# A planned encoder kernel: new costs and a rule for the shared port in the clock that lays out the order

## The chip, the cores and the metric

The kernel runs on one core of a Trainium2 chip. The metric is the device time in microseconds of one execution; three runs of the kernel before gave 1139.76, 1140.32 and 1140.52, the median is 1140.32. A core has TensorE (PE, matmuls, with a queue of its own for weight loads), VectorE (DVE), ScalarE (ACT), GpSimd (POOL) and SyncE (SP, which here issues the DMAs and the transposes done by DMA). Each engine works through its own instructions in the order in which the program has them; engines wait for each other by semaphores.

## The reference

Two groups of 512 rows with 1024 columns, prompt and sample, go through two layers with the same weights. A layer norms its input, projects it once, feeds two mixers and projects their gated outputs back:

```python
h = rmsnorm(x, g_norm) * (1.0 + scale[:, None, :]) + shift[:, None, :]
proj = h @ w_in
qa, ka, va, ga, qb, kb, vb, gb = jnp.split(proj, idx, axis=-1)
qa = rope(...) * (HEAD_DIM ** -0.5); ka = rope(...)
for window, dilation in DILATED_PATTERNS:          # (128,1), (512,4), (2048,16)
    o_p, lse_p = dilated_attention(qa, ka, va, window, dilation)
    ...
ya = oa.reshape(B, S, A_WIDTH) * jax.nn.silu(ga)   # 8 heads of 64, softmax-merged patterns
yf = retention_direction(qf, kf, vf, lg_f, False)  # 4 heads, key 64, value 128
yb = retention_direction(qf[:, ::-1], ..., True)[:, ::-1]
r = yf + yb
r = r * lax.rsqrt(jnp.mean(r * r, axis=-1, keepdims=True) + EPS)
yr = r.reshape(B, S, R_WIDTH) * jax.nn.silu(gb)
out = jnp.concatenate([ya, yr], axis=-1) @ w_out
return x + gate[:, None, :] * out
```

A last rmsnorm follows the second layer. The inputs are float32. The kernel keeps that precision by splitting each operand into a high and a low part and multiplying three times (high·high, high·low, low·high).

## The kernel before

**Tiles.** The input projection is cut into items: P*i* (queries and keys of attention pair *i*, two heads), V*i* (its values), G*i* (a gate, eight of them), R*i* and W*i* (queries/keys and values of two retention heads). ORDER0 and ORDER1 (lines 31 and 32) fix the order of items in the two layers; this is the main flow. An item's product is a 128x512 tile in PSUM (`banks`) for each group b, made of 24 matmuls `hT,wH` and `hT,wL`. At the end of a layer stands the output projection: for each block of 128 rows, 8 parts k in the order 0, 1, 4, 5, 6, 7, 2, 3, each with the split yT (left) and wo (right), 48 matmuls `wo,yT` of 512 columns a block.

**Side work.** Beside the main flow some dozen generators wait for their turn:

- `rope` turns queries and keys and has SP write them into stacks (QS, KS, KL), 24 small DMAs per pair and group.
- `attn` (line 897) multiplies two score matmuls per tile and lets DVE take the mask and minimum (`sS<-banks,tabs`). `soften` (line 920) does the exponential on ACT, then on DVE a reciprocal, a scaling of it and, for two tiles, a TENSOR_SCALAR and a SCALAR_TENSOR_TENSOR that write the high and low half of the weights, pt. When both halves of a head are there, SP transposes the two pt into pT. `attn_pv` (line 950) multiplies pT with the values vn in 24 matmuls with 64 output rows, when both heads of a pair and group are transposed.
- `ret` and `r_out` (line 1030, line 1092) are the retention; `r_out` makes the norm (`nw`, `nwr`) with a chain of DVE operations between two groups of matmuls.
- `prepper` splits the next weights: ACT makes wH, GpSimd wL. `prep_o` does so for w_out: GpSimd makes the low part of wo, eight instructions of 128x1024 a layer.
- `splitter` makes yT: the high part on ACT, the low part on DVE, for each k and group.

**What sets the order.** The program order on each engine is the order of the Python calls. Every call goes through `Engine.__call__` (line 345 issues it), which also advances a rough clock: `Plan.note` (line 127) takes an operation's cost from `Engine.cost` (line 361), starts it when its engine, its inputs and its buffers are free in that clock, and notes the end. `Plan.pump` (line 174) runs between the main flow's groups of three matmuls: it lets every generator go on whose wish (a time in that clock) has come by the clock of PE, and else returns to the main flow. So the clock decides only what stands ahead of what; the chip's times are its own. `backlog()` lets no further score begin while the clock of DVE is over AHEAD = 3000 ns past that of PE. Buffers come from a heap of 48 tiles and are given out by the same clock; a tile's name in the trace is that of the first use of its buffer (so KS, KL or QS, sd or rsq may be names of other contents). The eight PSUM banks are five for the main flow and three for the rest.

## Time and profile before

| | |
|---|---|
| runs, median | 1140.32 us |
| profiled execution | 1136.72 us |
| its span, first to last instruction | 1135.0 us |
| mean granted TensorE clock | 0.976 |
| PE / DVE / ACT / POOL busy | 1056.1 / 853.1 / 391.4 / 201.1 us |
| instructions PE / DVE / ACT / POOL | 5443 / 1664 / 701 / 108 |

The profile gives for each engine its busy time and the intervals in which it stood, with what it waited for. A wait of PE is time that the program loses, if the work behind it isn't waiting for something else anyway; a wait of the other engines costs only where PE waits for them in turn. All instructions have line 345, because they are issued in one place, so groups are told apart by the names of their output and inputs.

### The profile page before, as it was taken

Reading aid. Unit: us, or ns where it says so; the run is one execution under the profiler, and the core shown is the slowest. Engines: PE = TensorE matmul, PEld = TensorE weight load, DVE = VectorE, ACT = ScalarE, POOL = GpSimd, SP = SyncE. Lnnn points to the kernel's source line nnn. Section 1 sums busy time; section 2 is a strip of 40 time slices with the busy share of each in tenths; the row PEclk is TensorE's granted clock in tenths of the full one; section 3 lists DMA queues with packets and bytes.
Section 4 is the critical chain, followed back from the end, with each engine's and each line's share of the span. In section 5 each row is a group of like instructions: output and inputs, shape, how many; then the busy total and the mean of one; then the engine's idle time right before and its main releaser. Section 6 shows DMA issues by size and latency. Waiting matters only on the chain.

```text
span 1135.0 us, 15575 instructions
## 1 busy us (share of the span) xinstructions
PE 1056.1 (93%) x5443; PEld 836.4 (74%) x5443; DVE 853.1 (75%) x1664; ACT 391.4 (34%) x701; POOL 201.1 (18%) x108
## 2 busy tenths in 40 slices
PE   5999999999999999939999999999999999995997
PEld 4677776677876778617888878877797777773886
DVE  5688766689768996885457798599858995598555
ACT  5454314223242333442233343424143232363101
POOL 3153002121012011260000111103203011233000
PEclk9999999999999999969999999999999999997999
DMA  9905977338775677793222396247742484765232
GB/s 282 325 20 142 179 183 245 113 105 181 160 180 196 165 159 158 188 234 91 92 81 69 91 200 137 75 103 170 144 122 51 118 179 104 201 143 154 75 111 74
DMA packets 256509, 164.53 MB, mean 145 GB/s; under 512 B 162032, under 2 KB 225808, under 8 KB 256432
## 3 DMA queue, kind: packets, MB, share of 16 engines
q1 hardware_dynamic: 256432, 163.55, 57.2%
q8 instruction: 43, 0.70, 0.3%
q14 instruction: 34, 0.28, 0.1%
HBM read 79.59 MB, written 8.40 MB: 78 GB/s over the span
## 4 chain that ended last, share of the span: by engine, by line
PE 54%; DVE 31%; SPq 5%; DMA 5%; issue 2%; ACT 2%; DVEq 0%; ACTq 0%
PE banks L345 54%; DVE pt L345 10%; SPq L345 5%; DVE sd L345 3%; DVE sS L345 3%; DVE sm L345 2%; DVE rc L345 2%; DVE rsq L345 2%; DVE th L345 1%; DVE yr L345 1%; DMA wa<-in_w_ada_dram 1%; DMA pT<-pt 1%; DVE nw L345 1%; DVE hT L345 1%; DMA raw<-in_w_in_dram 1%
## 5 line engine op out<-in xcount | busy, mean ns | idle before, releaser
L345 PE MATMUL banks<-hT,wH 128*128 128x512 f32 x1536 | 482.6, 395 | 3.5 <-DVE sm L345 2.3
L345 PEld LDWEIGHTS banks<-hT,wH 128*128 128x128 f32 x1536 | 288.1, 189 | 79.4 <-issue 15.0
L345 PE MATMUL banks<-hT,wL 128*128 128x512 f32 x768 | 300.4, 391 | 0.0
L345 POOL TENSOR_TENSOR wL<-raw,wH 128x512 fp32r<-128x512 f32 (+1 forms) x80 | 149.8, 1888 | 739.6 <-ACT wH L345 545.3
L345 PE MATMUL banks<-wo,yT 128*128 128x512 f32 (+1 forms) x792 | 182.1, 391 | 35.7 <-DVE yT L345 23.6
L345 PEld LDWEIGHTS banks<-wo,yT 128*128 128x128 f32 x792 | 148.0, 192 | 67.6 <-DVE yT L345 24.5
L345 PEld LDWEIGHTS banks<-hT,wL 128*128 128x128 f32 x768 | 145.2, 189 | 30.8
L345 PE MATMUL banks<-wH,hT 128*128 128x256 f32 x512 | 96.3, 283 | 0.0
L345 PEld LDWEIGHTS banks<-wH,hT 128*128 128x128 f32 x512 | 81.4, 191 | 1.9 <-issue 0.8
L345 ACT ACTIVATE wH<-raw 128x512 fp32r<-128x512 f32 (+1 forms) x80 | 61.3, 794 | 46.4 <-DMA raw<-in_w_in_dram 29.4
L345 PE MATMUL banks<-wL,hT 128*128 128x256 f32 x256 | 72.4, 283 | 0.0
L345 ACT ACTIVATE sS<-sS,sm 128x512 f32<-128x512 f32 x67 | 47.8, 714 | 67.8 <-DVE sm L345 67.7
L345 DVE SCALAR_TENSOR_TENSOR pt<-sS,sm,pt 128x512 f16<-128x512 f32 x67 | 64.8, 967 | 2.9
L345 DVE TENSOR_TENSOR res<-banks,gb 128x512 f32<-128x512 f32 (+1 forms) x33 | 22.1, 671 | 47.3 <-PE banks L345 47.3
L345 DVE TENSOR_SCALAR pt<-sS,sm 128x512 f16<-128x512 f32 x67 | 50.5, 753 | 7.7 <-DMA pT<-pt 6.2
L345 PE MATMUL banks<-sr,rv 128*128 128x512 f32 x167 | 48.9, 399 | 3.9 <-ACT sr L345 2.6
L345 DVE CUSTOM_DVE_ANT_0 sS<-banks,tabs 128x512 f32<-128x512 f32 x67 | 43.1, 685 | 10.8 <-PE banks L345 10.8
L345 POOL TENSOR_TENSOR wo<-rawo,wo 128x1024 fp32r<-128x1024 f32 x16 | 39.9, 2518 | 56.7 <-PE banks L345 28.8
L345 PEld LDWEIGHTS banks<-wL,hT 128*128 128x128 f32 x256 | 49.0, 191 | 1.0
L345 PE MATMUL banks<-pT,vn 128*64 128x512 f16 x384 | 46.2, 390 | 0.2 <-DMA vn<-vt 0.2
L345 ACT ACTIVATE sq<-xr 128x1024 bf16<-128x1024 f32 (+2 forms) x15 | 14.2, 943 | 88.0 <-issue 43.2
L345 PE MATMUL banks<-wa,siluT 128*32 128x128 f32 (+1 forms) x384 | 33.0, 397 | 8.7 <-DVE nst L345 6.0
(304 smaller groups left out, 1393.3 us busy)
## 6 DMA issues: line engine op xcount, KB each, us to landing
raw<-in_w_in_dram SPq DMA_DIRECT2D x56, 512.0 KB, 5.3
wa<-in_w_ada_dram SPq DMA_DIRECT2D x48, 512.0 KB, 4.9
rawo<-in_w_out_dram SPq DMA_DIRECT2D x16, 512.0 KB, 4.7
QS<-rs SPq DMA_DIRECT2D x96, 64.0 KB, 2.0
KL<-rc SPq DMA_DIRECT2D x74, 64.0 KB, 2.0
KS<-rs SPq DMA_DIRECT2D x70, 64.0 KB, 2.0
x1d<-xr SPq DMA_DIRECT2D x8, 512.0 KB, 2.9
xr<-x1d SPq DMA_DIRECT2D x8, 512.0 KB, 3.9
```

Of the source, the lines that this page charges most:

```text
L345: r = fn(*args, **kw)
```

## The change

`Engine.cost` gets other numbers: 512-column matmuls of TensorE 228 ns instead of 216 (64-row ones lose 14 ns); DVE operations from SBUF get 65 ns for each input that is one element wide; GpSimd 30 + 2.37 n instead of 150 + 2.1 n. And `note` gets a rule, `held`: an operation of DVE without a PSUM operand may not overlap in the clock with one of GpSimd, and the other way round; the later starts when the earlier has ended. AHEAD, the order of items, the buffers and the computations are as they were, and each engine has as many instructions as before.

```diff
--- before.py
+++ after.py
@@ -96,6 +96,7 @@
     def __init__(self):
         self.free = {"PE": 0.0, "DVE": 0.0, "ACT": 0.0, "POOL": 0.0, "SP": 0.0}
         self.dma = 0.0
+        self.port = {"DVE": [], "POOL": []}
         self.ready = {}
         self.last = {}
         self.slots = {}
@@ -124,7 +125,18 @@
         t = self.at(*tiles)
         return 0.0 if t <= self.free[eng] else t
 
-    def note(self, eng, cost, outs, ins, nbytes=0.0):
+    def held(self, eng, start, cost):
+
+        other = self.port["POOL" if eng == "DVE" else "DVE"]
+        for s, e in other:
+            if s < start + cost and e > start:
+                start = e
+        own = self.port[eng]
+        own.append((start, start + cost))
+        del own[:-64]
+        return start
+
+    def note(self, eng, cost, outs, ins, nbytes=0.0, port=False):
         part = eng == "SP" and outs[0].shape[0] < P
         outs = [k for a in outs for k in self.keys(a)]
         ins = [k for a in ins for k in self.keys(a)]
@@ -136,6 +148,8 @@
                 start = max(start, self.seen(eng, self.last.get(k)))
         if self.dead.intersection(outs + ins):
             raise RuntimeError("use of a spare buffer")
+        if port:
+            start = self.held(eng, start, cost)
         end = start + cost
         self.free[eng] = end
         if eng == "SP":
@@ -354,7 +368,9 @@
             nbytes = 0.0
             if self.name == "SP":
                 nbytes = outs[0].free_size() * outs[0].shape[0] * (2.0 / 290.0 if outs[0].dtype == F16 else 4.0 / 360.0)
-            self.plan.note(self.name, self.cost(op, outs, ins), outs, ins, nbytes)
+            psum = any(a.tensor.name.startswith("banks") for a in ins)
+            port = self.name == "POOL" or (self.name == "DVE" and not psum)
+            self.plan.note(self.name, self.cost(op, outs, ins), outs, ins, nbytes, port)
             return r
         return call
 
@@ -372,18 +388,21 @@
                     return max(4 * c, 60.0)
                 self.strip = out.offset // out.ap[0][0] // 32
                 return 27.0 if self.strip > last >= 0 else 4 * c
-            return 0.5 * c + 14.0 if out.shape[0] == 64 else c
+            return 0.5 * c if out.shape[0] == 64 else c + 12.0
         if self.name == "DVE":
             wide = [a for a in ins if a.free_size() > 1]
             fast = len(wide) <= 1 and not psum and op != "tensor_reduce"
             if op == "tensor_reduce":
                 n = wide[0].free_size()
-            return 66.0 + n * (0.53 if fast else 1.05) + (60.0 if fast and len(ins) > 1 and n > 64 else 0.0)
+            extra = 0.0
+            if n > 64 and not psum and (op == "scalar_tensor_tensor" or fast):
+                extra = 65.0 * sum(1 for a in ins if a.free_size() == 1) + (60.0 if fast else 0.0)
+            return 66.0 + n * (0.53 if fast else 1.05) + extra
         if self.name == "ACT":
             extra = sum(1 for a in outs[1:]) + sum(1 for a in ins if a.free_size() == 1)
             return (53.0 if psum else 93.0) + 93.0 * extra + 0.833 * n
         if self.name == "POOL":
-            return 150.0 + 2.1 * n
+            return 30.0 + 2.37 * n
         if op == "dma_start_transpose":
             return 1250.0 * n / 1024
         return 450.0 if any("dram" in str(a.tensor.name) for a in ins + outs) else 650.0
```

What moves, at three places. At the end of layer 0, TensorE's rows before (`hT,wH` are projections of the main flow, `KS,KL` here two scores of pair 3, `wo,yT` the first part of the output projection, and `pT,vn` the first of 24 matmuls of attn_pv for pair 3, group 0):

```order
L345 MATMUL banks<-hT,wL 128x512
L345 MATMUL banks<-KS,KL 128x512 x2
L345 MATMUL banks<-hT,wH 128x512 x2
L345 MATMUL banks<-hT,wL 128x512
L345 MATMUL banks<-hT,wH 128x512 x2
L345 MATMUL banks<-hT,wL 128x512
L345 MATMUL banks<-wo,yT 128x512 x6
L345 LDWEIGHTS vn
L345 MATMUL banks<-pT,vn 64x512
```

All other scores of pair 3, and attn_pv of pair 2, stand ahead of these rows. In the changed order the last projections are followed by two scores of pair 3, group 0, and attn_pv of pair 2, group 1, begins:

```order
L359 MATMUL banks<-hT,wH 128x512 x2
L359 MATMUL banks<-hT,wL 128x512
L359 MATMUL banks<-KS,KL 128x512 x2
L359 LDWEIGHTS vn
L359 MATMUL banks<-pT,vn 64x512
```

Behind its 24 matmuls stand 22 score matmuls of pair 3 (14, then 8 in rows with QS), and only then attn_pv of pair 3, group 0, whose first rows end this piece:

```order
L359 LDWEIGHTS vn
L359 MATMUL banks<-pT,vn 64x512
L359 MATMUL banks<-KS,KL 128x512 x14
L359 MATMUL banks<-QS 128x512
L359 MATMUL banks<-KL,QS 128x512
L359 MATMUL banks<-QS 128x512
L359 MATMUL banks<-KL,QS 128x512
L359 MATMUL banks<-QS 128x512
L359 MATMUL banks<-KL,QS 128x512
L359 MATMUL banks<-QS 128x512
L359 MATMUL banks<-KL,QS 128x512
L359 LDWEIGHTS vn
```

Before, all 16 score pairs of pair 3 stood among the projections; now four do, the first of them 62 matmuls ahead of the projections' end, and twelve stand behind it.

The same place on SP's queue, before (the first rows are the end of pair 3's stacks for group 1, 24 DMAs; those for group 0 stand further up, ahead of other loads):

```order
L345 DMA KS<-rs 32x512 x4
L345 DMA KS<-rc 32x512 x4
L345 DMA_TRANSPOSE pT<-pt 128x16x128 x4
L345 DMA_TRANSPOSE vn<-vt 128x16x128
L345 DMA rawo<-in_w_out_dram 128x1024 x3
L345 DMA_TRANSPOSE pT<-pt 128x16x128 x2
L345 DMA rawo<-in_w_out_dram 128x1024 x4
L345 DMA_TRANSPOSE pT<-pt 128x16x128 x3
L345 DMA rawo<-in_w_out_dram 128x1024
L345 DMA_TRANSPOSE pT<-pt 128x16x128
```

And now (the first rows are the end of 48 DMAs in a run, group 1's stacks and behind them group 0's, issued behind attn_pv of pair 2, group 0):

```order
L359 DMA KS<-sd 32x512
L359 DMA KS<-yr 32x512
L359 DMA rawo<-in_w_out_dram 128x1024
L359 DMA_TRANSPOSE vn<-vt 128x16x128
L359 DMA rawo<-in_w_out_dram 128x1024 x4
L359 DMA_TRANSPOSE pT<-pt 128x16x128 x2
L359 DMA rawo<-in_w_out_dram 128x1024 x2
L359 DMA_TRANSPOSE pT<-pt 128x16x128 x6
```

The four transposes ahead of vn (pair 2's) are gone from behind the stacks, and six stand in one run at the end.

At the end of layer 1, TensorE's rows before (the 36 `wo,yT` are the first six parts of the first block):

```order
L345 MATMUL banks<-hT,wH 128x512 x2
L345 MATMUL banks<-hT,wL 128x512
L345 MATMUL banks<-wo,yT 128x512 x36
L345 LDWEIGHTS vn
L345 MATMUL banks<-pT,vn 64x512
```

And now, to the end of the program:

```order
L359 MATMUL banks<-hT,wH 128x512 x2
L359 MATMUL banks<-hT,wL 128x512
L359 MATMUL banks<-hT,wH 128x512 x2
L359 MATMUL banks<-hT,wL 128x512
L359 MATMUL banks<-wo,yT 128x512 x360
L359 MATMUL banks<-wo,yT 128x256 x48
```

The 24 matmuls of attn_pv for pair 3, group 1, which parted the output projection into 36 and 324, now stand among the projections.

## Rows read from the trace of the kernel before

**Rows 1.** Page, busy time, share of the span, instructions:

```profile
PE 1056.1 (93%) x5443; PEld 836.4 (74%) x5443; DVE 853.1 (75%) x1664; ACT 391.4 (34%) x701; POOL 201.1 (18%) x108
```

**Rows 2.** Page, chain that ended last, by engine:

```profile
PE 54%; DVE 31%; SPq 5%; DMA 5%; issue 2%; ACT 2%; DVEq 0%; ACTq 0%
```

**Rows 3.** Waits of PE: us in total, times, longest us:

```profile
PE banks L345 <- DVE yT L345: 23.6, 2, 13.6
...
PE banks L345 <- DVE nwr L345: 7.1, 4, 2.6
...
PE banks L345 <- DVE sm L345: 3.5, 2, 2.3
...
PE banks L345 <- ACT sr L345: 2.6, 3, 1.3
```

**Rows 4.** Timeline of PE, both seams: start, length, operation, [idle before <-releaser]:

```profile
491.59 2.93 PE L345 MATMUL banks<-wo,yT 128*128 128x512 f32 x6 [12.07 <-ACT yT L345]
...
509.51 3.78 PE L345 MATMUL banks<-wo,yT 128*128 128x512 f32 x8 [10.04 <-DVE yT L345]
513.22 3.05 PE L345 MATMUL banks<-pT,vn 128*64 128x512 f16 x24
516.20 8.00 PE L345 MATMUL banks<-wo,yT 128*128 128x512 f32 x34
...
1035.66 4.54 PE L345 MATMUL banks<-wo,yT 128*128 128x512 f32 x11 [13.57 <-DVE yT L345]
```

**Rows 5.** Stages: us, PE, PEld, DVE, ACT, POOL busy (x), PEclk, DMA share, GB/s:

```profile
479.53:491.59 12.06, 0.00 (x0) 0.00 (x0) 6.87 (x15) 5.60 (x8) 3.81 (x2) 0.65 0.98 183
...
499.47:509.51 10.04, 0.00 (x1) 0.01 (x1) 9.86 (x12) 1.72 (x3) 6.30 (x5) 0.70 0.76 210
...
1022.09:1035.66 13.57, 0.00 (x0) 0.00 (x1) 13.32 (x14) 3.79 (x7) 8.27 (x4) 0.64 0.32 61
...
233.81:237.20 3.39, 3.39 (x8) 2.71 (x9) 3.35 (x6) 0.00 (x0) 0.00 (x0) 0.51 0.24 58
```

**Rows 6.** Timeline of PE within layer 0, columns as in rows 4:

```profile
399.72 0.62 PE L345 MATMUL banks<-hT,wH 128*128 128x512 f32 x2
...
400.40 0.62 PE L345 MATMUL banks<-hT,wH 128*128 128x512 f32 x2
```

**Rows 7.** Groups of POOL by form: busy us, mean ns, idle before:

```profile
L345 POOL TENSOR_TENSOR wL<-raw,wH 128x512 fp32r<-128x512 f32 x48 | 69.5, 1470 | 262.8 <-ACT wH L345 137.3 <-PE banks L345 33.3 <-DVE sr L345 29.8
L345 POOL TENSOR_TENSOR wo<-rawo,wo 128x1024 fp32r<-128x1024 f32 x16 | 39.9, 2518 | 56.7 <-PE banks L345 28.8 <-DVE sm L345 15.3 <-ACT wo L345 10.5
```

**Rows 8.** Tile pt: ns min/median/max, first and last start:

```profile
L345 DVE TENSOR_SCALAR pt<-sS,sm x67: 474/486/2651, 95.4 to 1032.4; 128x512 f16<-128x512 f32 x67
L345 DVE SCALAR_TENSOR_TENSOR pt<-sS,sm,pt x67: 750/752/2771, 96.0 to 1032.9; 128x512 f16<-128x512 f32 x67
```

**Rows 9.** Timelines of POOL and DVE at the end of layer 0:

```profile
487.78 12.28 POOL L345 TENSOR_TENSOR wo<-rawo,wo 128x1024 fp32r<-128x1024 f32 x5 [10.50 <-ACT wo L345]
...
492.92 0.15 DVE L345 RECIPROCAL sm<-sm 128x2 f32<-128x2 f32 x1
...
497.85 2.76 DVE L345 SCALAR_TENSOR_TENSOR pt<-sS,sm,pt 128x512 f16<-128x512 f32 x1
```

**Rows 10.** Timeline of SP's queue, a stack and transposes:

```profile
428.16 2.49 SPq L345 DMA_DIRECT2D QS<-rs  x4
...
441.27 9.96 SPq L345 DMA_TRANSPOSE pT<-pt  x4
```

**Rows 11.** DMA issues: KB each, median us to landing:

```profile
QS<-rs SPq DMA_DIRECT2D x96, 64.0 KB, 2.0
...
pT<-pt SPq DMA_TRANSPOSE x64, 4.8
```

**Rows 12.** Groups of DVE by form: busy us, mean ns, idle before:

```profile
L345 DVE CUSTOM_DVE_ANT_0 sS<-banks,tabs 128x512 f32<-128x512 f32 x67 | 43.1, 685 | 10.8 <-PE banks L345 10.8
...
L345 DVE RECIPROCAL sm<-sm 128x2 f32<-128x2 f32 x64 | 10.1, 157 | 2.6 <-ACT sS L345 1.0 <-ACT th L345 0.9 <-ACT y L345 0.8
```

## The prediction

> **What bounds the kernel now.** I read the busy shares first. TensorE is busy 1056.1 us of the span of 1135.0, VectorE 853.1, GpSimd 201.1 [rows 1]: the kernel is bound by TensorE's work, and the change removes none of it. What can move is the time in which TensorE stands, some 79 us with the start. The chain that ended last has 54% on PE but 31% on DVE and 5% each on SP's queue and on DMAs [rows 2]; so in a third of the span TensorE is at the mercy of VectorE's order. The list of TensorE's waits then says where. The largest are for yT, the split operand of the output projection: 23.6 us in two waits on DVE [rows 3], and 12.07 us in one on ACT [rows 4]. The rest lies in the midst of the layers: nwr (the norm of retention) 7.1 us in four waits, sm 3.5, sr 2.6 [rows 3].
>
> The timeline and the table by stage place the long ones. At the end of layer 0 TensorE stands for 12.07 us up to 491.59 and for 10.04 up to 509.51, at the end of layer 1 for 13.57 up to 1035.66 [rows 4]. In the latter two DVE is busy for 9.86 and 13.32 us, with GpSimd beside it for 6.30 and 8.27 [rows 5]. Behind a stop TensorE is granted about half of its clock (1.2 of 2.4 GHz): 0.51 in the 3.39 us behind an nwr wait at 231 us, with eight matmuls where 0.227 us each would allow 15, so 1.6 us lost [rows 5, 6]. The spacing of 0.227 is read from the steady rows: three matmuls from 399.72 to 400.40 [rows 6].
>
> The seams' price from the same rows: layer 0 has 12.07 + 10.04 of standing, and matmuls at half clock: six in 2.93 and eight in 3.78 (0.51 and 0.48 apart, after 0.39 for the last one) lose 1.7 + 1.8. That is 25.6. Layer 1 has 13.57, and eleven in 4.54 (0.415 apart) lose 2.1: 15.7 [rows 4].
>
> Why is DVE late there? GpSimd's products (wo and wL) take 2518 and 1470 ns [rows 7]. Softening's two wide operations, both from SBUF, take 486 and 752 ns at the median, but up to 2651 and 2771 [rows 8]. The timeline shows one of them at 2.76 beside a row of wo, while a reciprocal beside the same row takes 0.15 [rows 9]. So the shared port that the change speaks of is real.
>
> **The change part by part.** No instruction is added or removed, none gets shorter. It alters four numbers of the clock that lays out the order, and adds a rule to it. The new numbers are nearer to the trace: TensorE 0.228 us for 512 columns (0.216 before; rows: 0.227), GpSimd 1.243 for 512 columns against 1470 ns, 2.457 for 1024 against 2518; the one-wide operand puts softening's operations at 462 and 669 ns against 486 and 752. The rule says that a DVE operation without a PSUM operand and a GpSimd operation never overlap. All of the effect is in what now stands ahead of what; I price it at three places.
>
> *End of layer 0.* Here the order gets worse. The 24 matmuls attn_pv(2,1), and 12 of the 16 score pairs of attention pair 3, stood among the projections; now they stand behind the last of these, in the rows shown above. Counted with 0.227, and 3.05 us for 24 attn_pv matmuls [rows 4], the projections end 24 × 0.227 + 3.05 = 8.5 us earlier, at 471.0 instead of 479.5. But pair 3's stacks (24 small DMAs per group) are now issued for both groups in one run behind attn_pv(2,0), group 1 first. That point is 150 matmuls, 34.0 us, ahead of the projections' end: 437.0. At 0.62 us an issue [rows 10] the first half of group 0's stack is the 36th: 437.0 + 22.3 + 2.0 to land [rows 11] = 461.3. Its first scores stand 62 matmuls ahead of the end, at 456.9, and TensorE waits 4.4 us. Fourteen matmuls and a gate later, at about 466, DVE starts four softenings, pair 3's two ahead of pair 2's last two. One is 2 × (0.486 + 0.752) [rows 8] + 0.157 for the reciprocal and as much for its scaling [rows 12] = 2.8 us; four end at 477, and one or two wo of 2.5 in their way make it 479.5 to 482; I take 481. Two transposes, 2.49 apart on SP's queue and 4.8 to land [rows 10, 11], bring attn_pv(2,1) to 488.3. TensorE stands from 475.4 + two scores to then, and all that follows is behind that in its order. From 491.4 DVE has 11 score operations at 0.685 = 7.5, six softenings = 16.8 and two small ones, 25.4 in all: 517, and with two to three wo between 519 to 524; I take 521. Two transposes 7.3, attn_pv(3,1) 3.05, then y and yT 2.1 and six matmuls 1.4: the first block of 48 output matmuls ends at 535. Before, it ends 30 matmuls after 516.20 [rows 4], at 523.0. So **+12 us**. The ends: if the first scores find their stack and no wo falls before attn_pv(2,1), 8 less (+4); if four more wo of 2.5 stand in DVE's way, +22.
>
> *End of layer 1.* Here it gets better. attn_pv(3,1) stood behind the first 36 output matmuls; now no attn_pv stands behind the projections at all, pair 3's scores being asked for 33 us of TensorE work sooner. Softening, which filled most of the 13.32 us of DVE in the standing window, is done by then. What is left is the last five wo, 12.6 us of GpSimd, with yT operations (0.7 alone, as the 0.685 of another 128x512 one [rows 12]) that each wait for one. Six matmuls use 1.36 us per yT where the pair of yT and wo needs 2.5: over four of them 4.6, less about 2 that begins before the projections end, plus 1 of half clock: 3.5 left of 15.7, **-12 us**. The ends: -14 (nothing left) and -5 (four alternations counted in full, 10).
>
> *Within the layers.* Of the four nwr waits two keep their place against the chain before them, the other two are given room: -1.5 of the 7.1. For sm and sr (6.1) I take a third, -2, and for the half clock behind one of the four stops -1.6: **-5**. Unknown on both sides: with all of these waits and four such stretches gone -19 at most, with each of the two kinds doubled in another place +13; I keep -12 and +6, as the waits are many and independent.
>
> Parts costed at nothing: the 64-row matmuls' 14 ns (TensorE's order is its only effect), the start (TensorE waits there for the first norms, ahead of any choice) and the end, where 324 output matmuls follow each other with DVE far ahead; if a later yT were late there, it would cost its wait in full.
>
> Sum: +12 - 12 - 5 = -5. Against the profiled execution's 1136.72 that is 1131.7; the median of the runs, 1140.32, lies 3.6 higher: **1135**.
>
> A rule speaks against the change. The Trainium skill ("SBUF — State Buffer", section "Who interferes with whom") states that a DVE instruction with at most one SBUF input, outside the two-port modes, does not contend with GpSimd. The trace agrees where a reciprocal ran in 0.15 us beside GpSimd while its neighbours took over 2 us. By that rule the new clock keeps operations waiting that the chip lets pass, and the time would be the first rival's.
>
> **Rivals.** First, *slower*: the rule charges too much. It holds every DVE operation without a PSUM operand for up to 2.457 us, reciprocals too, which the trace shows at 0.15 beside a wo [rows 9], and GpSimd in turn. DVE then looks busier than it is, the limit on DVE's backlog (AHEAD) lets pair 3's scores out later than needed, and TensorE, in order, stands behind them. For it: the late scores at the end of layer 0 are such a shift. Against: layer 1 shifts the other way. Price: three more wo of 2.5 us in layer 0, +20; two more in layer 1, -7; the rest 0: +13, 1153. It decides if attn_pv(2,1) starts after about 496.
>
> Second, *no change*: the standing only moves. TensorE's 1056 us are fixed, both layers have the same DVE work to do behind the last projections, and the waits within the layers come back elsewhere: +12 - 12 + 0, 1140.
>
> Third, *more gain*: layer 0 ends no later than before (+2), since the projections before it wait less and SP gets the stacks out sooner, layer 1 -13, within the layers -9: -20, 1120.
>
> **How the numbers follow.** The forecast (gain in layer 1, loss in layer 0, a little within) has 0.38, its own range 1129 to 1140; slower 0.30; no change 0.15; more gain 0.17. A measurement of this kernel can tell 0.2%, 2.3 us, from no change. Faster takes the third rival and 0.33 of the forecast's 0.38, 0.50; same its rival and 0.04 of the forecast, 0.19; slower the rest, 0.31. The range that leaves a tenth on each side is 1118 to 1151.
>
> **What would show it.** Right: two standing windows at the end of layer 0, the first closed by a transpose of pt for attn_pv(2,1), the end of the first 48 output matmuls some 12 us later than 523 counted from the projections' old end; a single stop of 2 to 5 us at the end of layer 1, closed by yT with wo beside it; nwr waits of about 5.5 us. Wrong: a first stop at layer 0 that ends before 482 (the stacks were not late), or one beyond 10 us at the end of layer 1 (wo, not softening, held DVE), or more waits within the layers than the 13 us of before.

## The result, and the profile after

The changed kernel takes 1179.99 us (median; 1175.90 to 1182.09) against 1140.04 for the kernel before beside it: a ratio of 1.0348 [1.0325, 1.0371]. It is slower, outside the range of 1118 to 1151. The profiled execution took 1182.09 us, with a span of 1179.9 where before had 1135.0: 44.9 us more.

The page's busy times, to be read against [rows 1]:

```profile
PE 1077.3 (91%) x5443; PEld 844.9 (72%) x5443; DVE 856.3 (73%) x1664; ACT 391.0 (33%) x701; POOL 200.7 (17%) x108
```

The work is the same. DVE and POOL differ from before by 3.2 and 0.4 us; PE shows 21 us more because more of its matmuls ran at half clock behind a stop (the granted clock over the span is 0.957; before 0.976). The waits of PE (us in total, times, longest), against [rows 3]:

```profile
PE banks L359 <- DMA pT<-pt: 31.9, 7, 16.1
PE banks L359 <- ACT sr L359: 14.4, 6, 5.1
PE banks L359 <- DMA wa<-in_w_ada_dram: 14.2, 9, 6.0
PE banks L359 <- DVE nwr L359: 5.8, 2, 3.2
PE banks L359 <- DVE sr L359: 5.6, 5, 2.0
...
PE banks L359 <- DVE yT L359: 3.9, 2, 2.6
PE banks L359 <- DVE sm L359: 2.6, 1, 2.6
```

yT has fallen from 23.6 to 3.9 and nwr from 7.1 to 5.8. In their place stand pT, the transposed softmax weights, on which no wait of TensorE ended before, and sr, the split scores of retention: 2.6 us on ACT before, 14.4 now, and 1.3 on DVE before, 5.6 now. Of the 14.2 for wa, 6.0 stand at the start, where before a wait of the same length was for nst on DVE. The timeline of PE tells where (start, length, operation, idle before and its releaser):

```profile
322.12 0.47 PE L359 MATMUL banks<-QS 128*128 128x512 f32 x1 [1.84 <-DMA QS<-rs]
324.65 0.76 PE L359 MATMUL banks<-QS,KL 128*128 128x512 f32 x1 [2.06 <-DMA KL<-rc]
330.56 1.95 PE L359 MATMUL banks<-sr,rv 128*128 128x512 f32 x3 [5.15 <-ACT sr L359]
...
496.08 0.61 PE L359 MATMUL banks<-KS,KL 128*128 128x512 f32 x2
...
513.10 1.06 PE L359 MATMUL banks<-pT,vn 128*64 128x512 f16 x4 [16.07 <-DMA pT<-pt]
515.66 4.42 PE L359 MATMUL banks<-pT,vn 128*64 128x512 f16 x19 [1.50 <-DMA pT<-pt]
...
537.29 1.06 PE L359 MATMUL banks<-pT,vn 128*64 128x512 f16 x4 [10.98 <-DMA pT<-pt]
...
887.38 1.95 PE L359 MATMUL banks<-sr,rv 128*128 128x512 f32 x3 [3.29 <-ACT sr L359]
889.12 1.05 PE L359 MATMUL banks<-KL,KS 128*128 128x512 f32 x2
891.68 1.95 PE L359 MATMUL banks<-sr,rv 128*128 128x512 f32 x3 [1.50 <-ACT sr L359]
...
900.23 1.95 PE L359 MATMUL banks<-sr,rv 128*128 128x512 f32 x3 [1.45 <-ACT sr L359]
```

The first three rows and the last four are new stops: the retention of the second pair, in layer 0 and in layer 1. In layer 1 TensorE does two score matmuls (KL, KS), waits, does three products (sr, rv), then the next two scores, with nothing else between. A round takes 4.3 us (887.38 to 891.68) where its five matmuls are worth 1.14 at [rows 6]' 0.227. The rows between are the end of layer 0, against [rows 4]. By stretches (us, busy time of PE, PEld, DVE, ACT, POOL, granted clock, DMA share, GB/s):

```profile
320.28:352.30 32.02, 18.32 (x61) 8.27 (x60) 14.76 (x20) 9.27 (x13) 4.81 (x3) 0.68 0.69 180
884.09:900.23 16.14, 8.40 (x16) 4.34 (x15) 5.99 (x9) 3.17 (x5) 1.28 (x2) 0.58 0.62 131
497.03:513.10 16.07, 0.00 (x2) 0.00 (x0) 15.47 (x20) 4.97 (x8) 7.14 (x3) 0.62 0.90 234
526.31:537.29 10.98, 0.00 (x1) 0.00 (x1) 10.56 (x25) 3.75 (x9) 1.21 (x1) 0.59 0.33 62
```

In the retention stretch of layer 1 no engine is full: DVE 5.99 of 16.14 us, ACT 3.17. TensorE is granted 0.58 there, near its half clock. It is a chain that goes round, not a busy engine. At the end of layer 0 DVE is full in both stops (15.47 of 16.07 us and 10.56 of 10.98), as it was before in two of the three at the seams [rows 5].

**Where the 45 us are.** I count as the loss of a stage the time between two fixed places of TensorE's work less what its matmuls between them take at steady spacing (0.227 us for 512 columns, half for one of attn_pv). So half clock counts as loss too. The end of a layer runs from the last gate but one to the end of the second block of the output projection; the retention stage begins with the end of the second pair's wide product (its values).

| stage | before | after | difference |
|---|---|---|---|
| second retention pair, layer 0 | 3.3 | 23.5 | +20.2 |
| end of layer 0 | 27.6 | 50.6 | +23.0 |
| second retention pair, layer 1 | -0.2 | 14.7 | +14.9 |
| end of layer 1 | 16.0 | 0.1 | -15.9 |
| all the rest | 41.5 | 44.3 | +2.8 |

The retention stage's other end isn't the next projection. Counted up to that projection's first matmul, it loses 0.5 before and 22.5 after in layer 0, and 0.0 and 15.0 in layer 1.

### The profile page after: what moved, and what is told of

Same layout as the page of the kernel before. It is cut to its first block, busy times and chain, and to the rows that moved or that the text cites. A ratio compares the mean times of both kernels' runs of the same rounds, so it can differ in the third digit from the quotient of the medians.

```text
span 1179.9 us, 15588 instructions
## 1 busy us (share of the span) xinstructions
PE 1077.3 (91%) x5443; PEld 844.9 (72%) x5443; DVE 856.3 (73%) x1664; ACT 391.0 (33%) x701; POOL 200.7 (17%) x108
## 4 chain that ended last, share of the span: by engine, by line
PE 54%; DVE 24%; SPq 11%; DMA 7%; issue 2%; ACT 1%; DVEq 0%; ACTq 0%
PE banks L359 54%; SPq L359 11%; DVE pt L359 8%; DMA wa<-in_w_ada_dram 2%; DVE sS L359 2%; DVE yr L359 2%; DVE th L359 2%; DMA raw<-in_w_in_dram 2%; DMA pT<-pt 2%; DVE rc L359 2%; DVE rs L359 1%; DVE sm L359 1%; DVE rsq L359 1%; DVE sd L359 1%; DVE sr L359 1%
## 5 line engine op out<-in xcount | busy, mean ns | idle before, releaser
L359 PE MATMUL banks<-wo,yT 128*128 128x512 f32 (+1 forms) x712 | 161.4, 385 | 5.7 <-DVE yT L359 3.9
L359 PEld LDWEIGHTS banks<-wo,yT 128*128 128x128 f32 x712 | 130.7, 189 | 32.8 <-DVE yT L359 4.8
L359 ACT ACTIVATE sS<-sS,sm 128x512 f32<-128x512 f32 x84 | 59.9, 714 | 71.4 <-DVE sm L359 71.3
L359 PE MATMUL banks<-pT,vn 128*64 128x512 f16 x384 | 53.5, 422 | 32.6 <-DMA pT<-pt 31.9
L359 DVE SCALAR_TENSOR_TENSOR pt<-sS,sm,pt 128x512 f16<-128x512 f32 x84 | 75.0, 893 | 5.1 <-PE banks L359 1.6
L359 PE MATMUL banks<-sr,rv 128*128 128x512 f32 x158 | 52.8, 437 | 20.0 <-ACT sr L359 14.4
L359 PEld LDWEIGHTS <-vn 128*64 128x64 f16 x384 | 23.9, 119 | 59.2 <-issue 44.3
L359 DVE CUSTOM_DVE_ANT_0 sS<-banks,tabs 128x512 f32<-128x512 f32 x84 | 54.4, 687 | 15.9 <-PE banks L359 15.2
L359 PEld LDWEIGHTS banks<-sr,rv 128*128 128x128 f32 x158 | 30.4, 202 | 35.5 <-ACT sr L359 19.1
L359 PE MATMUL banks<-wa,siluT 128*32 128x128 f32 (+1 forms) x384 | 37.5, 410 | 14.4 <-DMA wa<-in_w_ada_dram 14.2
```

What stands on the lines that cost most here:

```text
L359: r = fn(*args, **kw)
```

## The experiments

The table has every kernel that was run, with the losses of those four stages. "Apart" is what the order says of retention: how many TensorE matmuls stand between a score and its own product, in the four rounds of the first head of group 0. "pv" is the number of attn_pv matmuls that stand behind the layer's last projection.

| kernel | us | ratio to before | apart, layer 0 | loss | pv | end 0 | apart, layer 1 | loss | pv | end 1 |
|---|---|---|---|---|---|---|---|---|---|---|
| before | 1140.04 | | 24 37 44 45 | 3.3 | 48 | 27.6 | 28 31 32 18 | -0.2 | 24 | 16.0 |
| after | 1179.99 | 1.035 | 0 0 6 3 | 23.5 | 72 | 50.6 | 0 0 0 0 | 14.7 | 0 | 0.1 |
| pe_cost_only | 1160.06 | 1.017 | 25 32 33 13 | 4.2 | 72 | 39.3 | 25 28 29 18 | -0.1 | 0 | 0.2 |
| costs_only | 1184.35 | 1.039 | 2 5 29 15 | 30.7 | 72 | 40.8 | 25 28 29 18 | -0.1 | 0 | 4.7 |
| rule_only | 1161.79 | 1.019 | 37 19 26 27 | 0.1 | 96 | 61.2 | 16 19 53 39 | 0.3 | 24 | 13.3 |
| rule_holds_dve_only | 1145.48 | 1.006 | 13 16 17 6 | 14.1 | 48 | 29.6 | 21 17 5 3 | 7.9 | 0 | 0.1 |
| old_costs_ahead_2500 | 1156.11 | 1.014 | 25 28 29 6 | 5.9 | 48 | 44.3 | 4 7 8 6 | 14.6 | 0 | 1.5 |
| old_costs_ahead_2900 | 1119.77 | 0.982 | 24 37 44 45 | 4.8 | 24 | 10.7 | 79 34 20 21 | -0.1 | 24 | 13.9 |
| old_costs_ahead_1500 | 1115.15 | 0.979 | 24 37 44 42 | 5.6 | 24 | 16.5 | 46 31 20 21 | -0.1 | 0 | 0.3 |
| new_clock_5_weight_buffers | 1162.63 | 1.020 | 25 28 29 18 | 5.0 | 24 | 21.9 | 25 28 29 18 | -0.1 | 0 | 0.1 |
| new_clock_share_12 | 1133.74 | 0.996 | 4 5 8 3 | 13.7 | 24 | 16.1 | 22 25 26 18 | -0.2 | 0 | 0.1 |
| new_clock_share_11 | 1133.18 | 0.994 | 20 25 17 18 | 4.9 | 24 | 23.7 | 22 25 26 18 | -0.2 | 0 | 0.1 |
| new_clock_reserve_2 | 1150.10 | 1.010 | 0 26 5 3 | 11.8 | 24 | 16.9 | 0 0 0 0 | 14.9 | 0 | 1.0 |
| new_clock_pair3_unheld | 1230.94 | 1.082 | 0 0 6 3 | 20.4 | 48 | 55.0 | 4 7 8 12 | 21.5 | 72 | 37.9 |
| old_costs_retention_late_interleaved | 1137.25 | 0.998 | as before | 7.1 | 48 | 27.2 | 19 22 23 12 | -0.4 | 24 | 19.4 |
| old_costs_retention_alone_17 | 1143.31 | 1.004 | as before | 5.2 | 48 | 28.6 | 4 7 8 12 | 4.1 | 48 | 23.4 |
| old_costs_retention_alone_37 | 1144.13 | 1.005 | as before | 6.8 | 48 | 27.1 | 4 7 8 6 | 5.8 | 48 | 19.8 |
| old_costs_retention_alone_46 | 1147.31 | 1.007 | as before | 3.6 | 48 | 27.6 | 4 7 8 6 | 7.1 | 48 | 20.1 |
| old_costs_retention_alone_37_serial | 1153.78 | 1.012 | as before | 5.2 | 48 | 28.3 | 0 0 0 0 | 13.6 | 48 | 18.3 |
| old_costs_retention_alone_46_serial | 1167.14 | 1.024 | as before | 4.1 | 48 | 28.4 | 0 0 0 0 | 20.9 | 48 | 19.9 |

The last six have before's order on TensorE up to layer 1, so their layer 0 repeats one order: its end comes out within 1.5 us, its retention within 4. Differences below that are not read. A stage's loss is for whatever stands in it: the 21.5 of new_clock_pair3_unheld in layer 1 is mostly one wait of 14.8 for pT, and the 14.6 of old_costs_ahead_2500 stands in the stretch just behind and has 4.7 of pT in it. Nor do the four stages hold every loss. Against before, and by the spans of the profiled executions, everything else loses 26 us more in pe_cost_only, 20 in costs_only, 47 in new_clock_5_weight_buffers, 16 in new_clock_share_12 and new_clock_reserve_2, 11 in new_clock_share_11, 8 in rule_holds_dve_only, and within 7 of before in the others.

**The parts alone.** First theory: the loss lies where the main flow stands still for want of buffers, so that retention's second pair runs with nothing beside it, and at the end of layer 0. Against it: the rule is the loss (theory 2), or the new costs are, TensorE's above all (theory 3).

```diff
pe_cost_only (before, with):
+            return 0.5 * c if out.shape[0] == 64 else c + 12.0
costs_only (after, with):
+            port = False
rule_only: before's costs, with held() and port as in the change
```

> Only TensorE's two new numbers are kept, the other costs and the port rule are as before. In its order no run of retention matmuls stands without a projection between them; at the end of layer 0, 12 score matmuls and attn_pv(2,1) stand behind the projections, at the end of layer 1 no attn_pv does. Theory 1 (the loss is where the main flow stands still for want of buffers, so that retention of the second pair of heads runs with nothing beside it, and at the end of layer 0): 1132 to 1148, no waits of TensorE for sr above 3 us in sum, layer 1's end under 5 us. Theory 2 (the port rule is the loss, the costs are harmless): 1130 to 1142. Theory 3 (the new costs are the loss, TensorE's above all): over 1155.

> All four new costs, without the port rule. In its order 17 retention matmuls stand without a projection between them in layer 0 (37 in the changed kernel), none in layer 1; behind the projections of layer 0 stand 6 scores and attn_pv(2,1). Theory 1: about half of the changed kernel's loss in layer 0's retention (+10), +10 to +15 at the end of layer 0, -12 at the end of layer 1: 1140 to 1157. Theory 2: the loss is gone, below 1142. Theory 3: the loss stays, 1170 to 1185.

> The port rule with the old costs. In its order 9 retention matmuls stand alone in layer 0 and 8 in layer 1; behind the projections of layer 0 stand 28 scores and three attn_pv, those of pair 2 for both groups and pair 3's. Theory 1: small losses in retention, a larger one at the end of layer 0 than in the changed kernel (+25 to +40 against the kernel before), layer 1's end as before: 1160 to 1185. Theory 2: 1170 to 1185, spread over both layers. Theory 3: below 1150.

Measured: 1160.06, 1184.35 and 1161.79, ratios 1.0170 [1.0131, 1.0209], 1.0392 [1.0361, 1.0424] and 1.0193 [1.0168, 1.0217]. TensorE's numbers alone cost 12 us more than the first theory allowed, all costs 27 more; both fell where theory 3 had them. The rule alone fell where theory 1 had it, and theory 3 wanted it below 1150. So none of the three fits all of them. The parts don't add up: each lays out another order and loses in other places. The rule alone loses 33.6 us more than before at the end of layer 0. TensorE's numbers alone lose 11.7 more there and win 15.8 at the end of layer 1; the 26 that make them slower are spread over both layers and are not taken apart. In costs_only the largest wait is of a kind that nobody forecast; PE's timeline:

```profile
350.01 2.26 PE L359 MATMUL banks<-wa,siluT 128*32 128x512 f32 x6 [24.22 <-DMA wa<-in_w_ada_dram]
```

48 stack DMAs stand ahead of wa's load in one run on SP's queue, from 314.2 to 345.6 us, mostly 0.63 apart; so 24.2 of its retention loss of 30.7 is that queue, not retention.

**Is it the numbers, or any other order?** The clock's look-ahead is nudged with the old costs.

```diff
old_costs_ahead_2500 / _2900 / _1500 (before, with):
-AHEAD = 3000.0
+AHEAD = 2500.0   (2900.0; 1500.0)
```

> The kernel before, old costs and no port rule, with one number of the planner other than it was: AHEAD 2500 instead of 3000. In its order 31 retention matmuls stand alone in layer 0 and 57 in layer 1 (3 and 0 in the kernel before); behind the projections of layer 0 stand 14 scores. Theory 1: the same losses as in the changed kernel, without any of its edits, waits of TensorE for sr of 15 us or more: 1165 to 1195. Theories 2 and 3, in which the new numbers or the rule do the harm: within 1% of the kernel before, 1130 to 1150.

> The kernel before with AHEAD 2900 in place of 3000, old costs, no rule. In its order 3 and 7 retention matmuls stand alone, no score stands behind layer 0's projections, one attn_pv does there (two before) and one in layer 1 (as before). Theory 1: no stage gets worse, layer 0's end is shorter: 1125 to 1143. Rival (the order of the kernel before is the best of many, any nudge costs 15 us or more): 1152 or more.

> The kernel before with AHEAD 1500 in place of 3000. In its order 3 and 11 retention matmuls stand alone, no score and one attn_pv stand behind layer 0's projections, nothing behind layer 1's. Theory 1: as with 2900 (1119.8) without the 14 us at layer 1's end: 1100 to 1118. Rival (a limit so low starves DVE, so waits within the layers grow): 1125 or more.

Ratios 1.0143 [1.0113, 1.0173], 0.9823 [0.9792, 0.9854] and 0.9789 [0.9770, 0.9808]. A nudge of 3% in one constant is worth 1.8%, half of what the whole change did, the other way. 2500, at 1156.11, fell between the theory (1165 to 1195) and its rivals (up to 1150), 2900 came out 5 us below what was expected of it, 1500 inside. 1500 is the fastest of all, with one seam of 16.5 us left.

**Buffers and the rule, with the new clock.**

```diff
new_clock_5_weight_buffers (after): -NW = 6   +NW = 5
new_clock_share_12, _11 (after):    -NTURN = 10   +NTURN = 12 (11)
rule_holds_dve_only (after):
-            start = self.held(eng, start, cost)
+            s = self.held(eng, start, cost)
+            start = s if eng == "DVE" else start
new_clock_reserve_2 (after):
-                    pump(lambda: max(H.avail(1, 4, K_ROPE), B_IN.avail(1, 2)))
+                    pump(lambda: max(H.avail(1, 4, 2 if kind == "PQK" and i == 2 and b == 0 else K_ROPE), B_IN.avail(1, 2)))
```

> The changed kernel, all its costs and the rule, with five pairs of buffers set aside for split weights in place of six (NW 5). In its order the main flow no longer stops for buffers between the values of retention's second pair of heads and the next projection (0 and 6 retention matmuls alone there, 37 and 34 in the changed kernel), no score stands behind the projections of layer 0 (24 in the changed kernel) and one attn_pv does (three). Theory 1, by stages: layer 0's retention stop goes (-20 against the changed kernel), layer 1's too (-14), layer 0's end falls to 20 to 30 us (-22): 1118 to 1145. Rival (the new clock loses in any order, by waits spread over the layers): 1160 or more.

> The changed kernel, but the rule delays DVE alone in the clock, never GpSimd. In its order 40 and 30 retention matmuls stand alone in the two layers, no score stands behind layer 0's projections, two attn_pv do, as in the kernel before; none in layer 1. Theory 1, by stages: both retention stops stay (+20 and +12 against the kernel before), layer 0's end is as before (25 to 33 us), layer 1's end is gone (-14): 1152 to 1172. Rival (GpSimd's holds of up to 15 us in the clock are the harm): 1145 or less.

> The changed kernel with twelve buffers instead of ten in the share of pt, pT, vt and vn (NTURN 12). In its order 37 retention matmuls stand alone in layer 0 and none in layer 1, no score behind layer 0's projections and one attn_pv, none in layer 1. Theory 1: layer 0's retention stop stays (+20 against the kernel before), layer 0's end 20 to 30 us, layer 1's two losses gone (-14): 1140 to 1162. Rival: 1165 or more.

> The changed kernel with eleven buffers in the share of pt, pT, vt and vn (NTURN 11). In its order no retention matmul of the second pair stands alone in either layer, no score and one attn_pv stand behind layer 0's projections, nothing behind layer 1's. Theory 1: retention stages under 7 us each, layer 0's end 10 to 22 us, layer 1's end under 3: 1112 to 1132, faster than the kernel before. Rival (the new costs and the rule are worse in themselves): 1145 or more.

> The changed kernel, but the main flow asks for a reserve of 2 halves in place of 6 at one place, the first projection of pair 2 for group 0. Its order is the changed kernel's up to there. That projection now goes on, and the next one, group 1's, stands still instead: 60 retention matmuls of pair 1 for both groups, with attn_pv, stand there without a projection; 26 in layer 1. No score behind layer 0's projections and one attn_pv, none in layer 1. Theory 1 (want of buffers): the loss of layer 0's retention moves one projection later and keeps 10 to 25 us; layer 0's end falls to 10 to 25; layer 1's stop 5 to 12: 1135 to 1160. Rival (the loss there comes from late stacks or weights on the DMA queue, not from buffers): the retention stage under 8 us.

1162.63 (1.0201 [1.0172, 1.0230]), 1145.48 (1.0059 [1.0037, 1.0082]), 1133.74 (0.9955 [0.9939, 0.9971]), 1133.18 (0.9943 [0.9920, 0.9966]) and 1150.10 (1.0098 [1.0082, 1.0113]). Four of the five came out off what was expected: one weight buffer less 18 us above it and where its rival had it (1160 or more), the rule on DVE alone 7 below it and at its rival's edge (1145), the shares 6 below and 1 above; only the reserve of 2 fell inside. With one weight buffer less, which leaves its room to the rest, both retention stops and over half of layer 0's end are gone, as expected (5.0, -0.1 and 21.9); but two waits took their place:

```profile
PE banks L359 <- DVE nwr L359: 19.3, 4, 6.1
PE banks L359 <- DVE KL L359: 17.4, 1, 17.4
```

The two shares, with new costs and rule kept, are 0.5% faster than before. So the new clock need not make the kernel slower. With the rule on DVE alone no score stands behind layer 0's projections, and their end loses 29.6 in place of 50.6. With the reserve of 2 the projections got through at layer 0 and the end of the layer fell from 50.6 to 16.9, but a retention loss of 11.8 stayed, with 7.4 more just behind.

**Pair 3's scores sooner.** Second theory, for the end of layer 0: pair 3's scores stand behind the projections since DVE's backlog holds them.

```diff
new_clock_pair3_unheld (after):
-                    yield lambda: max(plan.at(qs, ks, kl), B_BG.avail(), backlog(),
+                    yield lambda: max(plan.at(qs, ks, kl), B_BG.avail(), 0.0 if p == 3 else backlog(),
```

> The changed kernel, but the scores of attention pair 3 are let out without regard to the limit on DVE's backlog. Up to the last gates of layer 0 its order is that of the changed kernel, the same 37 retention matmuls alone included; behind layer 0's projections stand no scores (24 in the changed kernel) and two attn_pv (three). In layer 1, 17 retention matmuls stand alone, and 8 scores and three attn_pv behind the projections. Theory 1: up to 490 us as the changed kernel, layer 0's end 25 to 33 us instead of 51, layer 1's retention stop smaller, layer 1's end 12 to 25 us: 1160 to 1178. Rival (layer 0's end is long since wo and yT alternate with DVE at the port, wherever the scores stand): layer 0's end over 42 us.

1230.94 (1.0816 [1.0793, 1.0839]), the slowest, 53 us above what was expected. All scores of layer 0 now stand ahead of the projections' end, and that end still loses 55.0 (12 of it ahead of the last projection). The theory fell; its rival, which had over 42, stands. The stretch of its longest stop, up to attn_pv of pair 3:

```profile
512.60:541.16 28.56, 0.00 (x0) 0.03 (x1) 23.98 (x22) 7.21 (x11) 18.54 (x9) 0.54 0.52 115
```

DVE does 22 operations in 23.98 us beside nine of GpSimd's (seven wo, two wL). What holds TensorE here is softening, one DVE operation beside each of GpSimd's, with all scores of that layer done.

**Retention: alone, or one score at a time?** Up to here the count of retention matmuls that stand alone (37 and 34 after, 3 and 0 before) was the theory. The next six kernels test it on before's order, changed at one place of layer 1.

```diff
all six (before, in ret, ahead of its wait for stacks and values):
+        if (l, r, b) == (1, 1, 0):
+            yield lambda: 0.0 if "wide" in have else INF
behind its products:
+            have.add(("ret", l, r, b, h))
alone_17: "wide" is set right behind the wide product (interleaved: as the next projection begins)
alone_37, alone_46 (main flow, behind it):
+                    plan.wait(lambda: ("ret", 1, 1, 0, 0) in have)   (46: head 1)
..._serial (37: head 0; 46: both heads):
-                if m == 4 or m - n > RLAG:
+                if m == 4 or m - n > (0 if (l, r, b, h) == (1, 1, 0, 0) else RLAG):
```

> The kernel before (old costs, no rule), identical on TensorE up to layer 1's wide product (values of the second retention pair). There group 0's retention is made to wait until that product and the first third of the next projection's half have been issued, so it is as late as in the changed kernel, but interleaved with projections: only 6 retention matmuls stand alone. Theory (standing alone is what costs): retention stage of layer 1 loses at most 2 us more than before, total 1137 to 1146. Rival (lateness of retention costs, alone or not): 8 us or more in that stage, 1148 or more.

> The same with group 0's retention let go right at the end of the wide product: 17 of its matmuls stand alone ahead of the next projection. Theory: four rounds of score, VectorE, ScalarE, VectorE, product at 4.3 us each where their matmuls need 1.1, as in the changed kernel: the stage loses 9 to 13 us more than before. Behind layer 1's projections stand now 48 attn_pv matmuls of pair 3 where 24 stood, which is worth 0 to 12 more by the other kernels' layer ends: 1149 to 1166 in all. Rival (a stop here is given back later, since VectorE's work behind it gets room): total within 5 us of the interleaved kernel.

> The same, and the main flow is held behind the wide product until head 0 of group 0 is done: 37 retention matmuls stand alone, as in layer 0 of the changed kernel. Theory: two heads' rounds, 15 to 25 us lost in the stage (34 matmuls lost 15 in layer 1 of the changed kernel, 37 lost 20 in layer 0); with the same layer end as the 17: 1155 to 1178. Rival: within 5 us of the interleaved kernel.

> The same, held until both heads of group 0 are done: 46 stand alone. Theory: 20 to 30 us lost in the stage, 1158 to 1183, and not less than with 37. Rival: within 5 us of the interleaved kernel, or a loss that does not grow from 17 to 46.

Measured 0.9982 [0.9961, 1.0003], 1.0044 [1.0026, 1.0061], 1.0045 [1.0020, 1.0071] and 1.0074 [1.0047, 1.0100]. Being late costs nothing, being alone costs 4.1, 5.8 and 7.1 us: it grows with the count, but is about a third of what was expected, and at most half of the 14.7 after. The three times lie 6, 11 and 11 us below what was expected. The theory fell in its size. What differs shows in PE's timeline of alone_37:

```profile
840.63 0.39 PE L345 MATMUL banks<-QS 128*128 128x512 f32 x1
840.86 0.39 PE L345 MATMUL banks<-QS,KL 128*128 128x512 f32 x1
841.77 0.49 PE L345 MATMUL banks<-sr,rv 128*128 128x512 f32 x1 [0.53 <-ACT sr L345]
844.04 1.08 PE L345 MATMUL banks<-sr,rv 128*128 128x512 f32 x2 [1.77 <-DVE sr L345]
...
845.77 3.11 PE L345 MATMUL banks<-sr,rv 128*128 128x512 f32 x9
```

Three scores go ahead, and nine products then run without a wait. In the changed order each product stands right behind its own score. The last two kernels keep the same matmuls alone and change this only.

> The kernel with 37 retention matmuls alone in layer 1, with one thing more: in head 0 of group 0 no score may be issued ahead of the product before it (RLAG 0 in place of 2 for that head), as the changed kernel's order has it in layer 1, where no buffer is free for a second score. The 20 matmuls of that head are the same, alone as before; only their order is score, product, score, product in place of three scores ahead. Theory (each round waits out the whole chain score, VectorE, ScalarE, VectorE, product: 3.3, 1.5, 1.5, 1.5 us at half clock in the changed kernel, 16.14 us for 16 matmuls worth 3.6): the stage loses 13 to 18 us more than before where 37 with scores ahead lost 6; in all 1150 to 1160 with the same layer end. Rival (something else in the changed order made its stop long, as late decay tables or stacks): the stage stays within 3 us of that 6, total 1142 to 1148.

> The kernel with 46 alone, with both heads of group 0 one score at a time. Theory: eight such rounds, 22 to 30 us lost in the stage, 1158 to 1172 in all (if the layer end is as with 46). Rival: as for the other, 1144 to 1151.

Ratios 1.0124 [1.0102, 1.0146] and 1.0235 [1.0217, 1.0253]; both times are within what was expected. The stage loses 13.6 instead of 5.8, and 20.9 with 4.2 more just behind instead of 7.1 with 1.3. Counted up to the next projection, the six kernels lose 0.0, 4.5, 6.2, 8.4, 14.0 and 25.2, the changed one 15.0. PE's timeline of the 37 in a row of single rounds:

```profile
851.10 1.95 PE L345 MATMUL banks<-sr,rv 128*128 128x512 f32 x3 [1.50 <-ACT sr L345]
...
855.40 1.95 PE L345 MATMUL banks<-sr,rv 128*128 128x512 f32 x3 [1.49 <-ACT sr L345]
...
859.64 1.95 PE L345 MATMUL banks<-sr,rv 128*128 128x512 f32 x3 [1.44 <-ACT sr L345]
```

These are the changed kernel's rows of layer 1 again: 1.95 us of products at half clock behind 1.5 of standing, 4.3 apart. So layer 1's stop is shown: it is made by the order score, product, score, product with nothing between. In layer 0 no kernel tests it by itself. There the first two rounds have the same order (0, 0), but the stop begins with 3.9 us of waits for stacks (QS, KL) and 5.15 for the first sr. Along PE's rows about 10 of the 23 us are lost up to the first product, 9 in the rest of that head's four rounds and 4 behind them.

## Why the prediction was wrong

**The step that failed: "Within the layers", -5 with ends of -12 and +6.** Without the two ends of a layer, the measured difference is +37.9 (20.2 + 14.9 + 2.8). The step priced the waits that before's profile shows and asked of each whether the change lets it go. For nwr that did well: 5.8, forecast 5.5. For sm and sr it took a third off 6.1; sm came out at 2.6, but sr at 20.0 (14.4 on ACT, 5.6 on DVE). A new order can stop where there was hardly a wait to price, and retention's second pair cost +20.2 and +14.9. The text did name waits doubled in another place, +13, and took +6 of it because the waits are many and independent; these two stops are not, they are the same place of the program in both layers. Its own sign of being wrong, more waits within the layers than the 13 us of before, came true: nwr, sm and sr make 28.4 (22.8 without sr on DVE, which the 13 left out).

The stop of layer 1 could have been read from the changed order ahead of any run: there stand, between layer 1's wide product and the next projection, 20 retention matmuls in the order 2, 3, 2, 3 with nothing between, where before had 28, 31, 32 and 18 others. The price was in before's trace as well, in the durations of DVE and ACT: a round goes through two DVE operations and ACT's split between them, which take 0.68 and 0.69 us on DVE and 0.63 on ACT there (the last two rows of the changed kernel's DVE timeline below show the two on DVE, at 0.69); TensorE stands for part of that and does its five matmuls at half clock.

The reason why the scores can't go ahead lies in the planner: a score asks for three half buffers (line 1052 of the kernel before). In the changed order the planner has three or four whole buffers empty there, but it sets three of them aside for weights still to be loaded and split, so a second score finds none until a product has given its own back. Taking out that line's reserve leaves the order as it is, and taking out its backlog leaves these rounds as they are; with one weight buffer less the rounds stand 25 and more apart again (18 the last) and the stop is gone.

**End of layer 0: +12 forecast, +23.0.** The mechanism was right. The projections end, two scores follow, and TensorE stands until a transpose of pt for attn_pv(2,1), then again for attn_pv(3,0). The first scores waited 0.57, not 4.4 for their stacks. From the projections' end at 496.1 to attn_pv(2,1) are 17.0 us, where the sum had 488.3 - 475.4 = 12.9; from there to the end of the first 48 output matmuls at 568.0 are 54.9, where it had 535 - 488.3 = 46.7. The first, 4.1 more than forecast, is mis-sized in one term: four softenings with "one or two wo of 2.5 in their way". POOL's timeline shows five of them while DVE softens from 487.8 to 509.3:

```profile
489.26 2.54 POOL L359 TENSOR_TENSOR wo<-rawo,wo 128x1024 fp32r<-128x1024 f32 x1 [30.28 <-ACT wo L359]
493.68 2.40 POOL L359 TENSOR_TENSOR wo<-rawo,wo 128x1024 fp32r<-128x1024 f32 x1 [1.88 <-ACT wo L359]
497.53 4.79 POOL L359 TENSOR_TENSOR wo<-rawo,wo 128x1024 fp32r<-128x1024 f32 x2 [1.45 <-ACT wo L359]
504.78 2.34 POOL L359 TENSOR_TENSOR wo<-rawo,wo 128x1024 fp32r<-128x1024 f32 x1 [2.46 <-issue]
```

And DVE's timeline: first the five of this stretch that were held, then the two operations of a round of retention in layer 1:

```profile
489.47 2.62 DVE L359 TENSOR_SCALAR pt<-sS,sm 128x512 f16<-128x512 f32 x1
...
493.71 2.92 DVE L359 SCALAR_TENSOR_TENSOR pt<-rsq,sm,pt 128x512 f16<-128x512 f32 x1
...
497.92 2.13 DVE L359 TENSOR_SCALAR sm<-sm 128x2 f32<-128x2 f32 x1
500.19 2.42 DVE L359 TENSOR_SCALAR pt<-sS,sm 128x512 f16<-128x512 f32 x1
...
504.96 2.44 DVE L359 TENSOR_SCALAR pt<-rs,sm 128x512 f16<-128x512 f32 x1
...
890.21 0.69 DVE L359 TENSOR_TENSOR yr<-banks,dtab 128x512 f32<-128x512 f32 x1 [2.17 <-PE banks L359]
891.66 0.69 DVE L359 TENSOR_TENSOR sr<-yr,sr 128x512 fp32r<-128x512 f32 x1 [0.76 <-ACT sr L359]
```

Against [rows 8] and 0.17 for the small one they lose 2.13, 2.17, 1.96, 1.93 and 1.95: 10.1 us, which with four times 2.8 gives 21.3 of the 21.5 that softening took. In this stretch one wo holds one DVE operation. The 8.2 us behind are not taken apart; the sum had no half clock there, and twice 24 attn_pv matmuls took 6.9 and 6.7 (1.50 and 1.28 of it waits) where it had 3.05.

**End of layer 1: -12 forecast, -15.9.** Right in mechanism; the stop of 3.5 that was left for the last wo did not come, the stage loses 0.1.

**The rivals.** "Slower" was the right side, and its price for layer 0's end (+20, three more wo) is near the +23.0. Its cause, the rule that charges too much, is not needed for a slow kernel: without it the new costs alone are as slow (1.0392, though 24.2 us of that is the one wait for wa), and with new costs and rule in another share of buffers the kernel is faster than before. Nor is the rule cleared at layer 0's end: alone it puts 28 score matmuls behind the projections and loses 61.2 there, and where it holds DVE alone none stands behind them and 29.6 are lost. Each of these kernels has another order elsewhere too, so how much of the +23.0 is the rule's stays open. A stop in retention was in no rival.

**What goes with the loss at a layer's end.** Over all kernels of the table the clock's accuracy does not sort the times. The pv columns nearly sort the two end columns: none behind the last projection loses 0.1 to 4.7 us, 24 lose 10.7 to 23.7, 48 lose 18.3 to 55.0, 72 lose 37.9 to 50.6, 96 lose 61.2. Counted from the last projection on, those with none lose 0.0. That is a regularity over orders that differ in more than this, not an experiment on it. Why old_costs_ahead_1500's planner falls on a good order and the changed one on a bad one stays open.

## What to carry to other kernels

When a change re-lays an order, read the new order for stops of its own before pricing the old waits: at each loop that goes from the bound engine over two others and back, count what stands between its halves (none here: 4.3 us a round instead of 1.14), and count what still stands behind the last independent work (a regularity here, not tested by itself). Such a planner turns a small truth in its costs into another order, not necessarily a better one: one constant moved by 3% gave -1.8%, by 17% gave +1.4%, so the range of such a prediction must be at least that wide, and the largest gain on record, -2.1%, came from moving that constant alone.

## What the runs showed of the hardware

- A tiny DVE operation can be held like a wide one: TENSOR_SCALAR on 128x2 takes 0.17 us and took 2.13 beside a wo. A RECIPROCAL of that size passed in 0.15 beside one [rows 9], and none of the 64 in the kernel before took over 0.166. The Trainium skill ("SBUF — State Buffer", section "Who interferes with whom") counts tensor_scalar among the operations that can take the shared pair, and exempts an operation with at most one SBUF input outside the two-port modes; the two groups agree (ns, min/median/max):

```profile
L345 DVE RECIPROCAL sm<-sm x64: 146/157/166, 95.0 to 1030.8; 128x2 f32<-128x2 f32 x64
L345 DVE TENSOR_SCALAR sm<-sm x64: 169/170/2421, 95.2 to 1031.0; 128x2 f32<-128x2 f32 x64
```

- Half clock (1.2 of 2.4 GHz) lasted through a whole run of short rounds: the granted clock was 0.58 from 884 to 900 us in the changed kernel and 0.55 from 848 to 862 us in old_costs_retention_alone_37_serial. Three products took 1.95 us in each round at 1.5 us of standing; nine without a stop between them took 3.11.
- In costs_only 48 small DMAs in a run on SP's queue were 31 us in which nothing else on it was issued, and one load behind them cost TensorE 24.22 us.
